# Expert stage with a fixed order on three engines, weights split five pieces ahead, halves summed and experts scattered in pairs

## The chip, the cores and the metric

The kernel runs on one core of one Trainium2 chip. The metric is the device time of one execution in microseconds; the kernel before took 2125.14 us, the median of three runs (2124.23 to 2125.2).

## The reference, cut to what matters

Two transformer blocks run one after the other on 512 tokens of width 1024. The change touches the expert layer of the first block: 16 experts, each of which takes the 64 tokens with the highest affinity to it.

```python
cap = CAPACITY_FACTOR * S // N_EXPERTS                     # 64
aff = softmax(h @ w_router)                                # per token over experts
g, idx = lax.top_k(aff.transpose(0, 2, 1), cap)
xin = h[idx]                                               # (16, 64, 1024)
a = xin @ w_gate[e];  u = xin @ w_up[e]                    # 1024 x 1024 each
y = (silu(a) * u) @ w_down[e]
y = y * g
x = x + g2 * zeros.at[idx].add(y)                          # scatter back
```

The other parts are a Fourier and windowed attention mixer before it, and behind it two further layers with other attention forms and convolutional feed-forward networks.

## The kernel before

Everything is fp32. A product that must keep fp32 accuracy on TensorE is made of fp32r matmuls on split operands: an operand is copied to `hi` (ScalarE, a cast to fp32r) and the residue `lo` is the original less `hi` (VectorE). `pieces` (L350) does this for a streamed weight: it takes a chunk of 1 MB (2048 columns on 128 partitions) that `fetch` (L337) brings from HBM on SP's queue into a raw buffer, and yields it in two pieces of 128 x 1024, each split into `whi` (L374) and `wlo` (L375). The split buffers come from the lists `parts` and by default from the pool `wp` (three); the raw buffers from the list `rings`.

The expert stage is `phase_b` (L1003). `_moe_order` gives the order of the 48 products: for each expert e a gate product (g), an up product (u) and a down product (d), as g0 u0 g1 d0 u1 g2 d1 u2 and so on, and at the end g15 u15 d14 d15. A product (`prod`, L1080) has eight pieces k of the contraction, two halves of 512 output columns in two PSUM banks, and a stationary operand of 128 columns: 64 with `hi` and 64 with `lo` of the expert's 64 rows. So the output has 128 rows, the upper half and the lower half of which are to be added. For seven of the pieces there are four matmuls (L1095: two halves, `whi` and `wlo`). Piece 5 (`WHOLE`) is not split: it is multiplied in fp32 (L1092), and its raw buffer is held until TensorE has used it.

Between the pieces of a product stand hooks, each a step of some other work: `gather` fetches the rows of the next expert by an indirect transfer, transposes them (L1072) and splits them; `activ` transposes the gate and up rows of an expert with a duplicating matmul (L1125), applies silu (L1128), multiplies (L1129, tile `sg`) and splits to `act`; `scatter` multiplies the rows `y` by the one-hot matrix `ph` (L1169) and adds the result into `x` (L1172). `first` (L1102) copies the output of a gate or up product to SBUF (L1110). `down` (L1140) scales the 128 output rows by the affinity and by g2 (`mt`, L1151), splits them to `y`, and builds `ph` (L1154), for each expert. As both halves of the 128 rows carry the same token index, the one-hot matmul adds them. The scatter goes over two experts at a time: eight steps of four matmuls and one add each.

All instructions are traced in program order, and a planner then orders those of each engine by its own estimate of when their inputs are ready. `pin` (L291) fixes an instruction behind the one traced before it on its engine; in this stage only the splits of the first three pieces are pinned. Up to the first down product there are three pairs of split buffers, then five. There are nine raw buffers (`NRAW` = 7 and two of `wp`).

Of the kernel before, what the change touches and what calls it, by code (L numbers as in the profile page):

```python
# [2 lines left out]

# [6 lines left out]
F32 = mybir.dt.float32  # L10
F32R = mybir.dt.float32r
# [4 lines left out]
OP = mybir.AluOpType  # L16
# [4 lines left out]
S = 512  # L21
D = 1024
EPS = 1e-6
NEG = -1e30
NE = 16
CAP = 64
# [1 line left out]
NF = DFF // 128  # L28
SEGS = ((0, 11), (11, 22))
CW = 2048  # L30
NPRE, NRAW, NPART = 6, 7, 2
WHOLE = (5,)
ROUTE = ((), (0,), (0, 1), (0, 1, 2, 3, 1, 2, 3, 2, 3))
SIDE = ()
NFIRST = 4
TAIL = 4
FILL = (0, 2, 2, 3, 3, 2, 2, 2, 0, 0, 0)
ODD = ("v0 v1 d0 d0 d0 d0 d0 d0 d0 d0 s0 d1 s0 d1 s0 d1 d0 d1 d1 s0 d1 s1 s0 d1 d1 s1 d1 s1 s1 s1").split()
# [221 lines left out]
    return {n: np.ascontiguousarray(v, dtype=f) for n, v in c.items()}  # L260

class Kernel:
# [737 lines left out]
    def phase_b(self, er, ep, after):  # L1003
        nc, tc, sp = self.nc, self.tc, self.sp
# [52 lines left out]
        nc.gpsimd.memset(xfull, 0.0)  # L1057
        nc.gpsimd.memset(afull, 0.0)

        def gather(e):  # L1060

# [16 lines left out]
                        nc.scalar.copy(xfull[:, e % 2, n, :CAP], t[:, k % 4])  # L1078
                yield

        def prod(name, stat, full, hooks):

            ps = [self.mm() for _ in range(2)]
            k = 0
            for j in range(4):
                for w in self.pieces(name, 1024, [i - 2 * j for i in WHOLE]):
                    for gen in hooks.get(k, ()):
                        next(gen, None)
                    for half in range(2):
                        sl = slice(half * 512, half * 512 + 512)  # L1090
                        if k in WHOLE:
                            nc.tensor.matmul(ps[half], full[:, WHOLE.index(k)], w[:, sl], start=(k == 0), stop=(k == 7))  # L1092
                            continue
                        for q in range(2):
                            nc.tensor.matmul(ps[half], stat[:, k], w[q][:, 0, sl],  # L1095
                                             start=(k + q == 0), stop=(k == 7 and q == 1))
                    k += 1
            return ps

        asb = {}  # L1100

        def first(t, e, hooks):  # L1102
            ps = prod(t, *xs[e], hooks)
            if t == "g":
                d = pw.tile([128, D], F32, name="ag", bufs=1)
            else:
                d = self.nrm.tile([128, D], F32, name="xn", tag="xn")
            asb[t, e] = d
            for half in range(2):
                nc.scalar.copy(d[:, half * 512:half * 512 + 512], ps[half])  # L1110

        act = {}

        def activ(e):
            a = [asb.pop((t, e)) for t in "gu"]
# [20 lines left out]
        ys = {}  # L1136

        def down(e, hooks):
            nonlocal pm, iota
            ps = prod("d", *act.pop(e), hooks)  # L1140
# [18 lines left out]
        def scatter(es, c):  # L1159

            for half in range(2):
                sl = slice(half * 512, half * 512 + 512)
                ps = self.av()
                n = 0
                for e in es:
                    y, ph = ys[e]
                    for q in range(2):
                        n += 1
                        nc.tensor.matmul(ps, ph[:, c * 128:(c + 1) * 128], y[:, q, sl], start=(n == 1),  # L1169
                                         stop=(n == 2 * len(es)))  # L1170
# [4 lines left out]
        def scatters(es):  # L1175
            for c in range(4):
                yield from scatter(es, c)

        gath, acts, none = gather(0), None, iter(())
        for _ in range(3):  # L1180
            next(gath)
        scat = none
# [12 lines left out]
        self.table()  # L1195
        nxt = after()
        for c in range(4):
            list(scatter([NE - 2, NE - 1], c))
            nxt(c)


# [587 lines left out]
```

## Time and profile before

| | |
|---|---|
| median of three runs | 2125.14 us (2124.23 to 2125.2) |
| the profiled execution | 2122.88 us |
| its span, first to last instruction | 2121.1 us |
| mean granted TensorE clock | 0.979 |
| TensorE matmul busy | 2006.7 us, 95% |
| VectorE busy | 1377.4 us, 65% |
| ScalarE busy | 1055.5 us, 50% |
| HBM | 169 GB/s over the span |

Busy time is the share of the span in which an engine has an instruction running; a matmul's end is modelled. In the rows, L and a number is the line of the kernel, "out<-in" are the names of tiles, x and a number counts instructions. An idle time stands before the arrow that names what ended it.

### The profile page before, as it was taken

The numbers are of one execution on the slowest core, as the hardware profiler recorded it, in microseconds if no ns is written. First come the engines' busy times: TensorE is split into PE (matmuls) and PEld (weight loads), VectorE is DVE, ScalarE is ACT, GpSimd is POOL, SyncE is SP. The second block draws the span as 40 slices with busy tenths as digits, with TensorE's granted clock in tenths as the row PEclk, the third lists the DMA queues.
The fourth block names the chain that finished last, engine by engine and source line by source line (L and its number), as shares of the span: only waits on it lengthen the run. The fifth ranks groups of instructions, "written<-read, shape, count | busy, mean of one in ns | idle before, by whom it ended". The sixth has DMA issues, their size and how long they took to land.

```text
span 2121.1 us, 24893 instructions
## 1 busy us (share of the span) xinstructions
PE 2006.7 (95%) x9331; PEld 1563.3 (74%) x9331; DVE 1377.4 (65%) x2328; ACT 1055.5 (50%) x1826; POOL 151.0 (7%) x146
## 2 busy tenths in 40 slices
PE   6889779999999999999999999999999989999998
PEld 5668657766666666787778888888887768888886
DVE  7676479888888888826856643553546776634653
ACT  3334368766777667526645433443425654423432
POOL 2003400000000010100101000001100010000001
PEclk9899989999999999999999999999999999999999
DMA  7744758999999997221123222222321023222221
GB/s 289 201 160 152 288 222 357 380 345 341 343 347 340 350 353 276 97 77 49 42 86 113 80 89 100 99 95 75 112 90 60 21 90 119 88 99 93 89 95 55
DMA packets 53932, 358.30 MB, mean 169 GB/s; under 512 B 6694, under 2 KB 7262, under 8 KB 14004
## 3 DMA queue, kind: packets, MB, share of 16 engines
q1 hardware_dynamic: 48148, 338.60, 42.7%
q0 software_dynamic: 5664, 18.12, 3.1%
q8 instruction: 73, 1.20, 0.2%
q14 instruction: 47, 0.39, 0.1%
HBM read 353.28 MB, written 4.46 MB: 169 GB/s over the span
## 4 chain that ended last, share of the span: by engine, by line
PE 82%; DVE 8%; issue 5%; ACT 3%; DMA 2%; POOL 0%; SPq 0%; DVEq 0%; POOLq 0%; ACTq 0%
PE mm L1095 15%; PE mm L384 13%; PE mm L385 13%; PE mm L386 13%; PE mm L1092 4%; PE tp L1125 2%; DVE wlo L375 2%; PE av L1169 2%; PE av L386 2%; PE av L384 2%; PE av L385 2%; PE tp L386 2%; PE tp L385 2%; PE tp L384 2%; PE mm L1220 1%
## 5 line engine op out<-in xcount | busy, mean ns | idle before, releaser
L375 DVE TENSOR_TENSOR wlo<-wraw,whi 128x1024 fp32r<-128x1024 f32 (+1 forms) x545 | 646.8, 1213 | 435.6 <-ACT whi L374 434.1
L374 ACT CAST whi<-wraw 128x1024 fp32r<-128x1024 f32 (+1 forms) x545 | 548.6, 1044 | 379.2 <-PE mm L385 148.5
L384 PE MATMUL mm<-hT_hi,whi 128*128 128x512 f32 (+1 forms) x960 | 375.9, 393 | 6.1 <-ACT whi L374 6.0
L385 PE MATMUL mm<-hT_lo,whi 128*128 128x512 f32 (+1 forms) x960 | 375.3, 392 | 0.4 <-DVE hT_lo L390 0.4
L386 PE MATMUL mm<-hT_hi,wlo 128*128 128x512 f32 (+1 forms) x960 | 374.6, 391 | 0.0
L384 PEld LDWEIGHTS mm<-hT_hi,whi 128*128 128x128 f32 x960 | 182.4, 191 | 48.8 <-ACT whi L374 6.8
L385 PEld LDWEIGHTS mm<-hT_lo,whi 128*128 128x128 f32 x960 | 182.4, 190 | 42.0 <-DVE hT_lo L390 1.6
L386 PEld LDWEIGHTS mm<-hT_hi,wlo 128*128 128x128 f32 x960 | 182.3, 190 | 40.5
L1095 PE MATMUL mm<-wlo,xs 128*128 128x512 f32 x448 | 164.6, 419 | 7.7 <-DVE wlo L375 7.7
L1095 PE MATMUL mm<-whi,xs 128*128 128x512 f32 x448 | 170.3, 429 | 0.4 <-ACT whi L374 0.4
L385 PE MATMUL mm<-wlo,hT_hi 128*128 128x512 f32 (+2 forms) x288 | 110.4, 384 | 1.1 <-DVE wlo L375 0.9
L384 PE MATMUL mm<-whi,hT_hi 128*128 128x512 f32 (+2 forms) x288 | 110.6, 386 | 0.0
L386 PE MATMUL mm<-whi,hT_lo 128*128 128x512 f32 (+2 forms) x288 | 109.4, 381 | 0.6 <-DVE hT_lo L390 0.6
L1095 PEld LDWEIGHTS mm<-wlo,xs 128*128 128x128 f32 x448 | 77.8, 190 | 42.0 <-DVE wlo L375 28.3
L1095 PEld LDWEIGHTS mm<-whi,xs 128*128 128x128 f32 x448 | 83.7, 191 | 26.8 <-issue 8.4
L1169 PE MATMUL av<-y,ph 128*128 128x512 f32 x256 | 84.6, 427 | 12.1 <-ACT y L389 11.3
L389 ACT CAST aT_hi<-cv 128x512 fp32r<-128x512 f32 x44 | 27.3, 620 | 117.0 <-DVE cv L1698 117.0
L1095 PE MATMUL mm<-wlo,act 128*128 128x512 f32 x224 | 81.1, 425 | 3.8 <-DVE wlo L375 3.6
L1095 PE MATMUL mm<-whi,act 128*128 128x512 f32 x224 | 81.8, 427 | 0.0
L1169 PEld LDWEIGHTS av<-y,ph 128*128 128x128 f32 x256 | 48.7, 192 | 38.6 <-ACT y L389 21.6
L1697 ACT ACTIVATE cv<-cv 128x512 f32<-128x512 f32 x44 | 27.8, 632 | 89.1 <-DVE cv L1694 89.1
L384 PE MATMUL av<-whi,aT_hi 128*128 128x512 f32 x176 | 69.3, 394 | 0.0
(487 smaller groups left out, 3319.4 us busy)
## 6 DMA issues: line engine op xcount, KB each, us to landing
wraw<-in_wts SPq DMA_DIRECT2D x310, 1024.0 KB, 5.6
wraw<-in_wts SPq DMA_DIRECT2D x8, 768.0 KB, 4.2
x<-in_x SPq DMA_DIRECT2D x4, 512.0 KB, 12.7
out<-x SPq DMA_DIRECT2D x4, 512.0 KB, 2.6
wraw<-in_wts SPq DMA_DIRECT2D x2, 832.0 KB, 5.4
bias<-t5scr POOLq DMA_DIRECT2D x8, 192.0 KB, 13.2
hd<-xn POOLq DMA_DIRECT2D x3, 512.0 KB, 3.2
mod<-md POOLq DMA_DIRECT2D x1, 1024.0 KB, 11.3
```

The source lines that it names most:

```text
L374: i1 = nc.scalar.copy(hi[:, :n], t[:, a:a + n])
L375: i2 = nc.vector.tensor_tensor(lo[:, :n], t[:, a:a + n], hi[:, :n].bitcast(F32), op=OP.subtract)
L384: mm(ps, a[0], b[0], start=start, stop=False)
L385: mm(ps, a[0], b[1], start=False, stop=False)
L386: mm(ps, a[1], b[0], start=False, stop=stop)
L389: self.nc.scalar.copy(hi, src)
L1092: nc.tensor.matmul(ps[half], full[:, WHOLE.index(k)], w[:, sl], start=(k == 0), stop=(k == 7))
L1095: nc.tensor.matmul(ps[half], stat[:, k], w[q][:, 0, sl], start=(k + q == 0), stop=(k == 7 and q == 1))
L1125: nc.tensor.matmul(pt[:, k * 128:(k + 1) * 128], src[:, f * 128:(f + 1) * 128], dup, start=True, stop=True)
L1169: nc.tensor.matmul(ps, ph[:, c * 128:(c + 1) * 128], y[:, q, sl], start=(n == 1), stop=(n == 2 * len(es)))
L1220: nc.tensor.matmul(ps[:, :W], lhs[:, i * 128:(i + 1) * 128], rhs[:, :W], start=True, stop=True)
L1697: nc.scalar.activation(u[0], u[0], AF.Silu)
```

## The change

The stage runs through a wrapper (`InOrder`) that pins every instruction of TensorE, VectorE and ScalarE: each of the three has the order in which the program is traced. A single stream of pieces (`feed`) now runs over all 48 products, and `piece` takes from it so that `ahead` pieces past the current one have been split: two until the first down product is done, then five, across the ends of products. The split buffers are then six pairs (three of `pm`, three of `wp`), the raw buffers seven.

A down product's two halves of 64 rows are summed: ScalarE copies the one half to the other's partitions (`ya`), VectorE adds. Two experts, an even and an odd one, stand in the upper and lower 64 rows of one tile `yt`. `pair` scales that tile (once, 1024 columns), builds one `ph` and splits one `y` for the two, in two steps that are hooks of the next up product. The scatter takes one or two pairs at a time (`GROUPS`), with two matmuls per pair and step. `activ` uses the `av` banks for its second half. The hooks move: `activ` to pieces 2 and 3 of the gate product, the scatter to 5 and 7, in the up product to 3 and 7 where no pair is being finished.

```diff
-NPRE, NRAW, NPART = 6, 7, 2
+NPRE, NRAW, NPART = 6, 5, 3
+AHEAD = 5
+GROUPS = {1: (0, 1), 3: (2, 3), 5: (4, 5), 6: (6,), 7: (7,)}
...
+        idxp, gp = (sp.tile([128, NE // 2], F32, name=n, bufs=1) for n in ("idxp", "gp"))
+        for i in range(2):
+            h = slice(i * CAP, i * CAP + CAP)
+            nc.vector.tensor_copy(idxp[h], idxT[h, i::2])
+            nc.vector.tensor_copy(gp[h], gT[h, i::2])
...
-        self.late = 3
...
+        self.nc = nc = InOrder(nc, self.pin)
+        order = _moe_order()
+        feed = (w for t, _ in order for j in range(4) for w in self.pieces(t, 1024, [i - 2 * j for i in WHOLE]))
+        queue = []
+        ahead = 2
+
+        def piece():
+            queue.extend(itertools.islice(feed, ahead + 1 - len(queue)))
+            return queue.pop(0)
...
-            k = 0
-            for j in range(4):
-                for w in self.pieces(name, 1024, [i - 2 * j for i in WHOLE]):
-                    for gen in hooks.get(k, ()):
-                        next(gen, None)
+            for k in range(8):
+                w = piece()
+                for gen in hooks.get(k, ()):
+                    next(gen, None)
...
-                pg, pu = self.tp(), self.tp()
+                pg, pu = (self.av(), self.av()) if g else (self.tp(), self.tp())
...
-                self.parts = ([(self.wp, 3)] * 3 + [(pm, NPART)] * NPART) * 8 * NE
-                del self.parts[(3 * NE - 4) * (8 - len(WHOLE)):]
+                self.parts = ([(pm, NPART)] * NPART + [(self.wp, 3)] * 3) * 8 * NE
+                ahead = AHEAD
                 iota = self.const_load(pm, "iota")
-            y = pm.tile([128, 2, D], F32R, name="y", bufs=2)
+            own, other = (slice(i * CAP, i * CAP + CAP) for i in (e % 2, 1 - e % 2))
+            if e % 2 == 0:
+                rows[e // 2] = pm.tile([128, D], F32, name="yt", bufs=1)
+            t = rows[e // 2]
             for half in range(2):
                 sl = slice(half * 512, half * 512 + 512)
-                t = pm.tile([128, 512], F32, name="mt", bufs=2)
-                nc.vector.scalar_tensor_tensor(t, ps[half], gT[:, e:e + 1], self.g2[:, sl], op0=OP.mult, op1=OP.mult)
-                self.split(y[:, 0, sl], y[:, 1, sl], t)
-            ph = pm.tile([128, S], F32R, name="ph", bufs=2)
-            nc.vector.tensor_scalar(ph, iota, idxT[:, e:e + 1], None, op0=OP.is_equal)
-            ys[e] = (y, ph)
+                a = pm.tile([128, 512], F32, name="ya", bufs=2)
+                nc.scalar.copy(a[own], ps[half][other])
+                nc.vector.tensor_tensor(t[own, sl], ps[half][own], a[own], op=OP.add)
...
+        def pair(p, n):
+            t = rows.pop(p)
+            y = pm.tile([128, 2, D], F32R, name="y", bufs=3)
+            ph = pm.tile([128, S], F32R, name="ph", bufs=3)
+            ys[p] = y, ph
+            for i in range(n):
+                sl = slice(i * D // n, (i + 1) * D // n)
+                nc.vector.scalar_tensor_tensor(t[:, sl], t[:, sl], gp[:, p:p + 1], self.g2[:, sl], op0=OP.mult, op1=OP.mult)
+                if i == 0:
+                    nc.vector.tensor_scalar(ph, iota, idxp[:, p:p + 1], None, op0=OP.is_equal)
+                    yield
+                self.split(y[:, 0, sl], y[:, 1, sl], t[:, sl])
+            yield
...
-        for t, e in _moe_order():
+        for t, e in order:
             if t == "g":
                 gath = gather(e + 1) if e + 1 < NE else none
-                first(t, e, {0: [gath], 1: [acts or none], 3: [acts or none], 4: [scat], 5: [scat], 6: [scat], 7: [scat]})
+                first(t, e, {0: [gath], 2: [acts], 3: [acts], 5: [scat], 7: [scat]})
             elif t == "u":
-                first(t, e, {1: [scat], 2: [gath], 3: [scat], 4: [gath], 5: [scat], 7: [scat]})
+                fresh = fin is not none
+                first(t, e, {1: [fin], 2: [gath], 3: [none if fresh else scat], 4: [gath], 5: [fin],
+                             7: [none if fresh else scat]})
+                fin = none
                 acts = activ(e)
             else:
-                down(e, {1: [acts], 3: [acts]} if e + 2 == NE else {})
-                list(scat)
-                scat = scatters([e - 1, e]) if e % 2 and e + 1 < NE else none
+                down(e, {2: [acts], 3: [acts], 4: [scat], 5: [scat], 6: [scat], 7: [scat]} if e + 2 == NE else {})
+                if e % 2:
+                    p = e // 2
+                    fin = pair(p, 2 if e + 1 == NE else 1)
+                    if p in GROUPS:
+                        list(scat)
+                        scat = scatters(GROUPS[p]) if e + 1 < NE else none
+        list(fin)
```

`InOrder` hands every call of `nc.scalar`, `nc.vector` and `nc.tensor` through and pins the instruction that comes back.

## Rows read from the trace of the kernel before

**Rows 1.** windows: busy us of PE, PEld, DVE, ACT, POOL; clock; DMA; GB/s
```profile
279.40:320.80 41.40, 41.34 (x167) 29.37 (x168) 36.16 (x36) 35.56 (x47) 2.74 (x3) 0.93 0.65 251
...
458.40:533.00 74.60, 71.03 (x306) 48.79 (x304) 63.63 (x72) 51.37 (x72) 2.36 (x2) 1.00 0.93 344
...
320.80:855.10 534.30, 512.67 (x2223) 359.38 (x2221) 465.02 (x527) 375.46 (x512) 22.72 (x14) 1.00 0.90 340
325.00:425.00 100.00, 98.22 (x445) 72.61 (x444) 93.27 (x107) 76.66 (x108) 3.48 (x3) 1.00 0.96 381
```

**Rows 2.** chain of waits over two experts: start us, us, engine, line, count
```profile
552.90 0.64 PE tp L1072 x8
...
569.52 0.73 DVE mt L1151
...
573.77 1.20 PE mm L1095 x4
...
577.84 0.93 PE av L1169 x4
...
579.24 1.72 PE mm L1092 x4
580.95 2.32 PE mm L1095 x10
...
587.47 1.34 PE tp L1125 x12
```

**Rows 3.** VectorE's timeline: start us, us, instructions, idle time before
```profile
559.95 6.99 DVE L375 TENSOR_TENSOR wlo<-wraw,whi 128x1024 fp32r<-128x1024 f32 x6 [1.51 <-ACT whi L374]
...
585.13 0.42 DVE L1129 TENSOR_TENSOR sg<-sg,tp 128x256 f32<-128x256 f32 x1 [1.07 <-PE tp L1125]
585.47 1.22 DVE L375 TENSOR_TENSOR wlo<-wraw,whi 128x1024 fp32r<-128x1024 f32 x1
586.60 0.42 DVE L390 TENSOR_TENSOR act<-sg,act 128x256 fp32r<-128x256 f32 x1
```

**Rows 4.** groups of instructions from 320.8 to 855.1: busy us, mean ns, idle us
```profile
L375 DVE TENSOR_TENSOR wlo<-wraw,whi 128x1024 fp32r<-128x1024 f32 x308 | 363.4, 1220 | 18.2 <-ACT whi L374 17.5
L374 ACT CAST whi<-wraw 128x1024 fp32r<-128x1024 f32 x309 | 306.5, 1051 | 22.0 <-PE mm L1095 21.3 <-DVE wlo L375 0.6
...
L1172 DVE TENSOR_TENSOR x<-x,av 128x512 f32<-128x512 f32 x56 | 38.3, 685 | 7.7 <-PE av L1169 7.6
...
L1151 DVE SCALAR_TENSOR_TENSOR mt<-mm,gT,row_g 128x512 f32<-128x512 f32 x30 | 21.1, 747 | 15.1 <-PE mm L1095 15.1
...
L389 ACT CAST y<-mt 128x512 fp32r<-128x512 f32 x30 | 18.1, 618 | 16.4 <-DVE mt L1151 16.1
...
L389 ACT CAST act<-sg 128x256 fp32r<-128x256 f32 x30 | 12.2, 406 | 17.0 <-DVE sg L1129 16.9
...
L1154 DVE TENSOR_SCALAR ph<-c_iota,idxT 128x512 fp32r<-128x512 f32 x16 | 7.2, 482 | 0.0
```

**Rows 5.** waits of SP's transfer queue from 320.8 to 855.1: total, times, longest
```profile
SPq L345 <- DVE wlo L375: 295.5, 125, 8.9
SPq L345 <- PE mm L1092: 119.9, 43, 5.4
```

**Rows 6.** groups of instructions, whole span, of the shapes nearest to the new ones
```profile
L457 DVE SCALAR_TENSOR_TENSOR x<-osb,rs_y,x 128x1024 f32<-128x1024 f32 x16 | 21.3, 1331 | 0.8
...
L1365 DVE TENSOR_TENSOR qT<-mm,c_ropeq 64x512 f32<-64x512 f32 x8 | 5.6, 694 | 1.0 <-ACT qT L1364 0.8
...
L1364 ACT COPY qT<-mm 64x512 f32<-64x512 f32 x8 | 4.6, 576 | 2.6 <-PE mm L386 2.5
```

**Rows 7.** timeline at the stage's end, VectorE and TensorE
```profile
855.12 1.41 DVE L1151 SCALAR_TENSOR_TENSOR mt<-mm,gT,row_g 128x512 f32<-128x512 f32 x2 [0.97 <-PE mm L1095]
...
856.57 0.49 PE L1169 MATMUL av<-y,ph 128*128 128x512 f32 x1 [1.26 <-ACT y L389]
```

**Rows 8.** transfers issued from 320.8 to 855.1, KB each, median us to landing
```profile
wraw<-in_wts SPq DMA_DIRECT2D x167, 1024.0 KB, 7.0
```

More of the change, by code (lines that the diff above doesn't have):

```diff
@@ L1 @@
+import itertools
 import math
@@ L260, in constants, with __init__, __getattr__, pinned @@
     return {n: np.ascontiguousarray(v, dtype=f) for n, v in c.items()}
+class InOrder:
+    class Engine:
+        def __init__(self, engine, pin):
+            self.engine, self.pin = engine, pin
+        def __getattr__(self, name):
+            op = getattr(self.engine, name)
+            def pinned(*a, **k):
+                ins = op(*a, **k)
+                self.pin(ins)
+                return ins
+            return pinned
+    def __init__(self, nc, pin):
+        self.nc = nc
+        self.scalar, self.vector, self.tensor = (self.Engine(e, pin) for e in (nc.scalar, nc.vector, nc.tensor))
+    def __getattr__(self, name):
+        return getattr(self.nc, name)
 class Kernel:
@@ L1058, in phase_b @@
         nc.gpsimd.memset(afull, 0.0)
+        plain = nc
+        self.nc = nc = InOrder(nc, self.pin)
[6 more added lines that the diff above has]
+            return queue.pop(0)
         def gather(e):
@@ L1079, in gather, with prod @@
                 yield
-        def prod(name, stat, full, hooks):
+        def prod(stat, full, hooks):
             ps = [self.mm() for _ in range(2)]
-            k = 0
-            for j in range(4):
-                for w in self.pieces(name, 1024, [i - 2 * j for i in WHOLE]):
-                    for gen in hooks.get(k, ()):
-                        next(gen, None)
[L1089 to L1097, printed above, removed]
+            for k in range(8):
+                w = piece()
+                for gen in hooks.get(k, ()):
+                    next(gen, None)
+                for half in range(2):
+                    sl = slice(half * 512, half * 512 + 512)
+                    if k in WHOLE:
+                        nc.tensor.matmul(ps[half], full[:, WHOLE.index(k)], w[:, sl], start=(k == 0), stop=(k == 7))
+                        continue
+                    for q in range(2):
+                        nc.tensor.matmul(ps[half], stat[:, k], w[q][:, 0, sl],
+                                         start=(k + q == 0), stop=(k == 7 and q == 1))
             return ps
@@ L1102, in first @@
         def first(t, e, hooks):
-            ps = prod(t, *xs[e], hooks)
+            ps = prod(*xs[e], hooks)
             if t == "g":
@@ L1136, in phase_b @@
         ys = {}
+        rows = {}
         def down(e, hooks):
-            nonlocal pm, iota
-            ps = prod("d", *act.pop(e), hooks)
+            nonlocal pm, iota, ahead
+            ps = prod(*act.pop(e), hooks)
             if pm is None:
@@ L1143, in down, with scatter @@
                 pm = self.pool(er, "b_m", side="right")
-                self.parts = ([(self.wp, 3)] * 3 + [(pm, NPART)] * NPART) * 8 * NE
-                del self.parts[(3 * NE - 4) * (8 - len(WHOLE)):]
+                self.parts = ([(pm, NPART)] * NPART + [(self.wp, 3)] * 3) * 8 * NE
+                ahead = AHEAD
                 iota = self.const_load(pm, "iota")
-            y = pm.tile([128, 2, D], F32R, name="y", bufs=2)
+            own, other = (slice(i * CAP, i * CAP + CAP) for i in (e % 2, 1 - e % 2))
+            if e % 2 == 0:
+                rows[e // 2] = pm.tile([128, D], F32, name="yt", bufs=1)
+            t = rows[e // 2]
             for half in range(2):
                 sl = slice(half * 512, half * 512 + 512)
-                t = pm.tile([128, 512], F32, name="mt", bufs=2)
-                nc.vector.scalar_tensor_tensor(t, ps[half], gT[:, e:e + 1], self.g2[:, sl], op0=OP.mult, op1=OP.mult)
-                self.split(y[:, 0, sl], y[:, 1, sl], t)
-            ph = pm.tile([128, S], F32R, name="ph", bufs=2)
-            nc.vector.tensor_scalar(ph, iota, idxT[:, e:e + 1], None, op0=OP.is_equal)
-            ys[e] = (y, ph)
-        iota = None
-        def scatter(es, c):
+                a = pm.tile([128, 512], F32, name="ya", bufs=2)
+                nc.scalar.copy(a[own], ps[half][other])
+                nc.vector.tensor_tensor(t[own, sl], ps[half][own], a[own], op=OP.add)
+        iota = None
+        def pair(p, n):
[11 more added lines that the diff above has]
+            yield
+        def scatter(ps_, c):
             for half in range(2):
@@ L1164, in scatter @@
                 n = 0
-                for e in es:
-                    y, ph = ys[e]
+                for p in ps_:
+                    y, ph = ys[p]
                     for q in range(2):
@@ L1169, in scatter @@
                         nc.tensor.matmul(ps, ph[:, c * 128:(c + 1) * 128], y[:, q, sl], start=(n == 1),
-                                         stop=(n == 2 * len(es)))
+                                         stop=(n == 2 * len(ps_)))
                 xc = self.x[:, c, sl]
@@ L1173, in scatter, with scatters @@
                 yield
-        def scatters(es):
+        def scatters(ps_):
             for c in range(4):
-                yield from scatter(es, c)
-        gath, acts, none = gather(0), None, iter(())
+                yield from scatter(ps_, c)
+        none = iter(())
+        gath, acts = gather(0), none
         for _ in range(3):
             next(gath)
-        scat = none
-        for t, e in _moe_order():
+        scat = fin = none
+        for t, e in order:
             if t == "g":
                 gath = gather(e + 1) if e + 1 < NE else none
-                first(t, e, {0: [gath], 1: [acts or none], 3: [acts or none], 4: [scat], 5: [scat], 6: [scat], 7: [scat]})
+                first(t, e, {0: [gath], 2: [acts], 3: [acts], 5: [scat], 7: [scat]})
             elif t == "u":
-                first(t, e, {1: [scat], 2: [gath], 3: [scat], 4: [gath], 5: [scat], 7: [scat]})
+                fresh = fin is not none
+                first(t, e, {1: [fin], 2: [gath], 3: [none if fresh else scat], 4: [gath], 5: [fin],
+                             7: [none if fresh else scat]})
+                fin = none
                 acts = activ(e)
             else:
-                down(e, {1: [acts], 3: [acts]} if e + 2 == NE else {})
-                list(scat)
-                scat = scatters([e - 1, e]) if e % 2 and e + 1 < NE else none
+                down(e, {2: [acts], 3: [acts], 4: [scat], 5: [scat], 6: [scat], 7: [scat]} if e + 2 == NE else {})
[6 more added lines that the diff above has]
+        list(fin)
+        self.nc = nc = plain
+        self.parts = []
         el.close()
@@ L1197, in phase_b @@
         for c in range(4):
-            list(scatter([NE - 2, NE - 1], c))
+            list(scatter(GROUPS[NE // 2 - 1], c))
             nxt(c)
```

## The prediction

> **What bounds the kernel now.** I read the page's engine shares first, then the windows, the chain of waits over two experts, VectorE's timeline and the groups of instructions, and last the waits of SP's transfer queue. By the table of the profile TensorE is busy for 95% of the span, but a matmul's end is modelled, so this says little; the expert stage has to be taken apart. It runs from 279.4 to 855.1 us; 41.4 us go to the first four products, and 534.3 us to the other 45, that is 35.6 us per expert (three products), with a steady 74.6 us for two experts [rows 1]. The granted clock is 1.00 (the 2.4 GHz level) from 320.8 us on and 0.93 on average before; nothing in the change bears on it.
>
> TensorE needs less than that. From the chain [rows 2]: ten matmuls of a product take 2.32 us, so 0.232 each; the four of an unsplit piece 1.72; four scatter matmuls 0.93; twelve duplicating matmuls 1.34; eight gather transposes 0.64. Per expert: 84 x 0.232 = 19.5, 3 x 1.72 = 5.2, 32 x 0.112 = 3.6, 0.6, and 16 scatter matmuls x 0.2325 = 3.7 (3.5 in this window, as the last pair comes later): 32.4 us. So 3.2 us per expert are waits. Where they lie, the chain shows: a product ends at 569.5, and the path runs over VectorE (the scaled rows mt, a weight residue, y, again a residue) to 573.8, where the next product goes on [rows 2].
>
> VectorE is next. Six residues in a row take 6.99 us, so one is 1.15 us when one follows another, although its own time is 1.22 [rows 3, 4]. The last overlaps its successor by some 0.07 to 0.1 us, so I take 0.60 for an add of 0.685 into x and 0.34 for a 256-column operation of 0.42 [rows 3, 4]. Per expert: 21 x 1.15 = 24.2; adds into x 56/15 x 0.60 = 2.2; mt 2 x 0.70, y's residue 2 x 0.65 (its form is that of the add) and ph 0.44 (0.48 less the overlap) = 3.1 [rows 4]; six 256-column operations 2.0: 31.5 us. The windows say 465.0 / 15 = 31.0 [rows 1]. Both engines lie within a tenth of 35.6, and since the lead of the split is short they lose time to each other in turn: VectorE stands idle when a product's end is awaited, and TensorE while VectorE catches up.
>
> The transfers are third: 340 GB/s over the window, 344 in steady state at 0.93 of the transfer engines' time, 381 at 0.96 in the best 100 us [rows 1]. SP stood 295.5 us waiting for a residue to free a buffer and 119.9 us for an unsplit piece's matmul [rows 5], so they are paced by buffers now, though not far from their own limit.
>
> **Scatter by fours, two experts in one set of rows.** In this window 7 pairs x 16 instead of 14 x 16 scatter matmuls: 112 x 0.2325 = 26 us off TensorE, 1.7 per expert, leaving 30.6. Adds into x fall from 56 to 32 in the window: 24 x 0.60 = 14 us off VectorE.
>
> **Summing the halves.** Per expert two ScalarE copies of 64x512 and two VectorE adds of 64x512 come in. The nearest rows are a 64x512 copy from PSUM at 0.576 and a 64x512 two-input operation from PSUM at 0.694 [rows 6]; fewer partitions do not make them shorter, so I take 0.60 in a row for the add. Bounds: 0.35 (what a 256-column one takes in a row) to 0.75 (mt). Per pair there remain one 128x1024 scaling, one ph, one residue: 1.33 as in the nearest row [rows 6], 0.44, 1.15 = 2.9, or 1.5 per expert. VectorE pays 1.2 + 1.5 = 2.7 instead of 3.1. With the adds into x (32/15 x 0.60 = 1.3): 24.2 + 1.3 + 2.7 + 2.0 = 30.2 us per expert. ScalarE goes up by 2 x 0.5 + 0.5 - 2 x 0.6 = 0.3 on 375.5 / 15 = 25.0 [rows 1]: no bound.
>
> **The lead.** With six split buffers, ScalarE can begin piece k+5 when TensorE is done with k-1, and it is ready 1.05 + 1.22 = 2.3 us later [rows 4]; TensorE gets there after 5 x 0.93 = 4.65 us. That leaves 2.4 us and more. At a product's end ScalarE's copies wait for TensorE as before, but five pieces are ready by then. This hides the 4.3 us hole of [rows 2]; most of the 3.2 us per expert can go.
>
> **The fixed order.** It has a price where VectorE and ScalarE hand one tile to and fro. Now a residue stands between the gated product and its low part: sg at 585.13, a residue at 585.47, act at 586.60 [rows 3]. After the change these two are neighbours: the ScalarE cast between (0.41 [rows 4]) is awaited, and the next piece's cast stands behind it on ScalarE (1.05), of which act covers 0.42. Twice per expert: 0.45 + 0.6 and, with a further small copy, 0.45 + 0.85: 2.4 us. What is queued behind on VectorE are the residues that TensorE will need five pieces on. So VectorE goes from 30.2 to 32.6 us per expert when it is the late one, and nothing when it is ahead. A second price: the scatter bank taken at step 5 of a gate product is one that the gated products used at step 3. If VectorE is late there (after an up product in which a finished pair costs it 2.9 us extra), TensorE waits for it; I put that at 3 us in two of four experts, bounds 0 and 4, and 30.6 + 1.5 = 32.1 is still below VectorE's 32.6.
>
> The rule that speaks against this is in the Trainium skill, TensorE: Matmul & The Clock Gate, section on the array's architectural detail: VectorE and ScalarE take their queue strictly in order. The trace agrees as far as it goes: the idle time before sg stands in one piece, with the residue that could have filled it behind it [rows 3]. By that rule alone each such wait is paid in full, which is the 32.6 above; without it the sum would be 30.6.
>
> **Transfers and buffers.** Raw buffers fall from 9 to 7, while the split empties them five pieces earlier; only the chunk with the unsplit piece is held until TensorE uses it. 340 GB/s x 534.3 us is 181.7 MB, 12.1 MB per expert. At 381 GB/s [rows 1] that is 31.8 us, at 381 / 0.96 = 397 it is 30.5, at 344 / 0.93 = 370 it is 32.7. A transfer lands 7.0 us after its issue [rows 8], with a new one every 3 us (169 in 534.3), so two or three of the seven buffers are under way: no stall of its own, but no room either.
>
> **The sum.** VectorE 32.6, transfers 30.5 to 32.7, TensorE 30.6 to 32.1 per expert, all within a few per cent. Before, 32.4 and 31.5 made 35.6. I take 33.2: 0.6 on the largest, a fifth of the 3.2 that was lost before. Gain (35.6 - 33.2) x 15 = 36 us. Against it: the first four products keep three split buffers and a lead of two, now with the act price: +2 (0 to 5). At the end the last pair passes ScalarE copy, add, add, scaling and cast (0.58 + 0.69 + 0.69 + 0.75 + 0.62 = 3.3 us [rows 4, 6]) before its first scatter matmul, where now it takes 1.45 (855.12 to 856.57 [rows 7]); 16 matmuls fewer give part back: +1.5 (0 to 3). The four small index copies lie in VectorE's wait for the first gather. Outside the stage nothing changes. Net -32.5 us. The profiled execution took 2122.9 us (span 2121.1 and 1.8 around it), so it would be 2090.4; the median of the runs lies 2.2 above it: 2093 us. A stage at 32.4 to 34.4 per expert gives 2080 to 2111.
>
> **Rivals.**
> TensorE alone bounds. If the lead absorbs every wait, an expert costs 31.2: 15 x 4.4 = 66, net -63, 2062 us. For it: 2.4 us of slack per piece. Against it: VectorE's 30.2 leaves 1.0 us for waits of which I count 2.4.
>
> Transfers bound. With seven buffers and bursts of three behind the held chunk they may not exceed 350 GB/s: 12.1 / 0.350 = 34.6, net -11, 2114 us; it decides once VectorE and TensorE fall below 34.6. For it: the share of 0.93 at only 344 GB/s. Against it: 381 over 100 us, and SP's waits for buffers. The Trainium skill, DMA: Bandwidth & Descriptors, Specifications, gives some 358 GB/s as the HBM limit of a core; by that it would be 33.8 us and 2102. The trace does not agree that this is a ceiling: 381 over 100 us.
>
> Slower: the fixed order makes TensorE wait in every gate product. If VectorE is more than two pieces late at step 5, TensorE stands for 4 us in each, loses the lead, and the act price is paid again by TensorE at the next up and down products (1.5 each): 30.6 + 7 = 37.6, +30 and +3.5, 2159 us. It decides from 35.6 - 30.6 = 5.0 us of waits per expert on. Against it: the up product that precedes a gate has only two of four pairs' finishing work.
>
> **Chances.** Forecast 0.59, TensorE alone 0.15, transfers 0.15, slower 0.11. About 0.2% (4 us) is what a measurement tells from none. The forecast's cases and TensorE's are all faster; a fifth of the transfers' case and some of the forecast's upper end come near none. Faster 0.84, same 0.05, slower 0.11. The range for eight in ten reaches from TensorE's case, 2060, to the poorer half of the transfers' one, 2121.
>
> **What would show it.** After the stage's start, L1095 no longer waits 3 to 4 us at a product's end; the period of two experts falls from 74.6 to about 66 us; VectorE's adds of halves are near 0.69 each; the transfers rise to some 370 to 385 GB/s; the idle time before VectorE's act and the residue after it grows. Wrong if VectorE has over 5 us of idle time per expert, if the residues wait for transfers, or if the stretch from the first down product's end to the last is above 525 us.

## The result, and the profile after

The changed kernel takes 2097.49 us (median of 4 runs, 2095.03 to 2099.54) against 2124.68 (4 runs, 2122.32 to 2125.2): ratio 0.9872, 95% interval [0.9857, 0.9888], so 27 us faster; 2093 was forecast, in a range of 2060 to 2121. The profiled execution took 2099.54 us with a span of 2097.8, 23.3 less than before. Cut at the same events as [rows 1], the span of after minus that of before is: up to the first matmul of the stage +1.5 (280.9 against 279.4; over the profiled executions of all the kernels here, this start lay between 276.4 and 285.2, so it says nothing of the change), first four products +3.0, the other 45 products -34.6, everything behind the last product +6.8.

In the rows PE is TensorE, PEld its weight loads, DVE VectorE, ACT ScalarE, POOL GpSimd and SPq the queue of transfers. The windows of after that answer to [rows 1]: start to end, then span of the window and busy us of TensorE, its weight loads, VectorE, ScalarE, GpSimd; granted clock, DMA share, GB/s. The first is the first four products, the second the other 45, the third four experts.
```profile
280.90:325.30 44.40, 43.12 (x168) 29.04 (x169) 36.18 (x35) 35.24 (x45) 2.30 (x2) 0.93 0.56 205
325.30:825.00 499.70, 474.51 (x2114) 353.51 (x2112) 445.34 (x479) 380.50 (x521) 28.69 (x20) 0.98 0.94 371
461.30:596.70 135.40, 129.28 (x577) 97.12 (x576) 121.09 (x131) 104.04 (x143) 6.79 (x4) 0.97 0.95 377
```
An expert takes 499.7 / 15 = 33.3 us; two take 67.7, not 74.6. VectorE works 445.3 / 15 = 29.7 of the 33.3, so it is idle for 3.6.

The groups of instructions of the same 499.7 us (count, busy us, mean ns, idle time before and what ended it) answer to [rows 4, 6]. L279 is the line of the wrapper that pins every call of the stage, so groups go by tiles.
```profile
L279 DVE TENSOR_TENSOR wlo<-wraw,whi 128x1024 fp32r<-128x1024 f32 x307 | 360.0, 1219 | 39.1 <-ACT whi L279 37.4
...
L279 DVE TENSOR_TENSOR x<-x,av 128x512 f32<-128x512 f32 x32 | 21.7, 680 | 0.0
...
L279 DVE TENSOR_TENSOR yt<-mm,ya 64x512 f32<-64x512 f32 x30 | 19.3, 682 | 0.2
...
L279 ACT COPY ya<-mm 64x512 f32<-64x512 f32 x30 | 16.0, 581 | 0.8 <-PE mm L279 0.4
...
L279 DVE TENSOR_TENSOR act<-sg,act 128x256 fp32r<-128x256 f32 x30 | 12.8, 425 | 14.1 <-ACT act L279 14.1
...
L279 DVE SCALAR_TENSOR_TENSOR yt<-yt,gp,row_g 128x1024 f32<-128x1024 f32 x7 | 8.9, 1276 | 0.0
```
The adds into x are 32 instead of 56, the copies and adds of halves cost 0.58 and 0.68 us, the scaling of a pair 1.28. Of VectorE's 54.4 us of idle time, 51.5 end with a cast of ScalarE (37.4 + 14.1): they hand tiles to each other, and one stands.

The waits of after in the same window (total, times, longest), for [rows 5] and against what was forecast of the scatter bank:
```profile
ACT xfull L279 <- DVE xs L279: 54.6, 14, 5.3
ACT act L279 <- DVE sg L279: 44.2, 30, 2.1
DVE wlo L279 <- ACT whi L279: 37.4, 49, 1.2
...
PE tp L279 <- ACT xn L279: 21.0, 9, 3.0
...
PEld av L279 <- ACT sg L279: 0.8, 2, 0.5
...
SPq L372 <- DVE wlo L279: 186.4, 99, 12.0
SPq L372 <- PE mm L279: 184.0, 42, 8.9
```
The first row was not foreseen; before the change the same wait, from 320.8 to 855.1, was
```profile
ACT xfull L1078 <- DVE xs L390: 8.1, 5, 1.6
```
`gather` splits the transposed rows (`xs`: a cast on ScalarE, a residue on VectorE) and then lets ScalarE copy one column group of the same PSUM tile to `xfull`. In the program that copy waits for the residue. In the fixed order the residue stands in VectorE's queue behind work that is late, and behind the copy in ScalarE's queue stand `y`, the next casts, and the copy of the up product's rows, `xn`. The chain of waits of after (start us, us, what) shows one passage; it is what has come in the place of [rows 2]'s hole at 569.5.
```profile
565.56 1.11 DVE yt L279
...
568.40 0.42 DVE xs L279
568.82 2.27 DVE wlo L279 x2
571.09 0.34 DVE xs L279
...
571.46 0.02 ACT xfull L279
...
572.52 0.76 ACT y L279
...
573.46 1.99 ACT whi L279 x2
575.45 0.49 ACT xn L279
...
575.99 1.16 PE tp L279 x8
```
TensorE lives on its five split pieces in the meantime, and then stands at the duplicating matmuls that read `xn`: 21.0 us in 9 places. The same passage two experts on, in the timeline (the idle time before in brackets) and in windows of 2 us:
```profile
644.59 1.31 PE L279 MATMUL tp<-c_dup,xn 128*128 128x128 f32 x8 [2.46 <-ACT xn L279]
...
642.00:644.00 2.00, 0.14 (x2) 0.00 (x0) 2.00 (x3) 2.00 (x4) 0.00 (x0) 1.00 1.00 377
644.00:646.00 2.00, 1.41 (x9) 1.41 (x10) 1.88 (x2) 2.00 (x5) 0.00 (x0) 0.87 1.00 414
646.00:648.00 2.00, 2.00 (x7) 1.61 (x7) 2.00 (x2) 1.20 (x2) 0.00 (x0) 0.50 1.04 434
648.00:650.00 2.00, 2.00 (x16) 2.00 (x15) 1.12 (x3) 1.27 (x3) 0.00 (x0) 0.78 0.99 410
```
After 2.46 us of standing the granted clock falls from 1.00 to 0.50 (1.2 GHz), and TensorE gets 7 matmuls done in those 2 us; the next 2 us, at 0.78, hold 16. This happens six times in the stage, and nowhere in the stage before the change.

The end of the stage, [rows 7], in the timeline of after (start us, us, instruction, idle time before):
```profile
826.47 1.30 DVE L279 TENSOR_TENSOR yt<-mm,ya 64x512 f32<-64x512 f32 x2
827.81 0.75 DVE L279 SCALAR_TENSOR_TENSOR yt<-yt,gp,row_g 128x512 f32<-128x512 f32 x1
828.14 1.80 POOL L1358 MEMSET qz<- 64x2048 f32 x1
828.48 1.74 DVE L279 TENSOR_SCALAR ph<-c_iota,idxp 128x512 fp32r<-128x512 f32 x1
...
830.37 0.76 PE L1227 MATMUL av<-y,ph 128*128 128x512 f32 x1 [5.04 <-DVE ph L279]
...
841.98 1.32 PE L462 MATMUL tp<-ident,xn 128*128 128x128 f32 x8 [1.49 <-DVE xn L476]
```
From the last product to the first scatter matmul 5.4 us pass (1.5 before), and to the first transposes of the next part 17.0, where before these are 10.2 us behind 855.1:
```profile
865.30 0.60 PE L435 MATMUL tp<-ident,xn 128*128 128x128 f32 x4
```
So all of the +6.8 arises here. For [rows 8]: 169 transfers of 1 MB (167 before), now with a median of 9.4 us to landing instead of 7.0. The transfer queue still stands for buffers, 186.4 us for residues and 184.0 for matmuls of a product.

### The profile page after: what moved, and what is told of

It reads as the page before. It is cut to its first block, busy times and chain, and to the rows that moved or that the text cites. A ratio compares the mean times of both kernels' runs of the same rounds, so it can differ in the third digit from the quotient of the medians.

```text
span 2097.8 us, 24799 instructions
## 1 busy us (share of the span) xinstructions
PE 1966.8 (94%) x9203; PEld 1554.2 (74%) x9203; DVE 1362.1 (65%) x2286; ACT 1060.8 (51%) x1835; POOL 153.3 (7%) x146
## 4 chain that ended last, share of the span: by engine, by line
PE 76%; DVE 10%; issue 6%; ACT 5%; DMA 3%; POOL 0%; SPq 0%; ACTq 0%; DVEq 0%; POOLq 0%
PE mm L279 13%; PE mm L411 13%; PE mm L412 13%; PE mm L413 13%; DVE wlo L279 3%; PE av L279 2%; PE av L413 2%; PE av L412 2%; PE av L411 2%; PE tp L411 2%; PE tp L413 2%; ACT whi L279 2%; PE tp L412 2%; DMA wraw<-in_wts 2%; PE mm L1289 1%
## 5 line engine op out<-in xcount | busy, mean ns | idle before, releaser
L402 DVE TENSOR_TENSOR wlo<-wraw,whi 128x1024 fp32r<-128x1024 f32 (+2 forms) x209 | 250.6, 1201 | 412.2 <-ACT whi L401 412.1
L279 DVE TENSOR_TENSOR wlo<-wraw,whi 128x1024 fp32r<-128x1024 f32 x336 | 393.9, 1219 | 46.1 <-ACT whi L279 44.3
L401 ACT CAST whi<-wraw 128x1024 fp32r<-128x1024 f32 (+2 forms) x209 | 214.8, 1030 | 356.5 <-PE mm L412 145.3
L279 ACT CAST whi<-wraw 128x1024 fp32r<-128x1024 f32 x336 | 333.1, 1050 | 15.8 <-PE mm L279 14.8
L412 PEld LDWEIGHTS mm<-hT_lo,whi 128*128 128x128 f32 x960 | 182.3, 190 | 41.2 <-DVE hT_lo L417 1.6
L279 PE MATMUL mm<-whi,xs 128*128 128x512 f32 x448 | 199.7, 446 | 2.3 <-ACT whi L279 2.3
L279 PE MATMUL mm<-wlo,xs 128*128 128x512 f32 x448 | 183.1, 409 | 4.0 <-DVE wlo L279 3.7
L279 PEld LDWEIGHTS mm<-wlo,xs 128*128 128x128 f32 x448 | 86.6, 193 | 36.5 <-DVE wlo L279 14.5
L279 PEld LDWEIGHTS mm<-whi,xs 128*128 128x128 f32 x448 | 86.8, 194 | 27.3 <-issue 6.2
L279 PE MATMUL mm<-whi,act 128*128 128x512 f32 x224 | 94.4, 422 | 0.0
L279 PE MATMUL mm<-wlo,act 128*128 128x512 f32 x224 | 89.3, 399 | 0.5 <-DVE wlo L279 0.5
L411 PE MATMUL tp<-whi,aT_hi 128*128 128x512 f32 x176 | 69.4, 395 | 0.0
```

The lines of the kernel that those rows point to most:

```text
L279: ins = op(*a, **k)
L401: i1 = nc.scalar.copy(hi[:, :n], t[:, a:a + n])
L402: i2 = nc.vector.tensor_tensor(lo[:, :n], t[:, a:a + n], hi[:, :n].bitcast(F32), op=OP.subtract)
L411: mm(ps, a[0], b[0], start=start, stop=False)
L412: mm(ps, a[0], b[1], start=False, stop=False)
```

## Experiments

Ratios are to the kernel before, with their 95% intervals; the medians of before beside them lay between 2122.27 and 2124.93. "Stage" is the stretch of the 45 products, cut as above. "Theory" and "rival" are the two outcomes set out before each run.

**1. The xfull copy first.** In `gather`:
```
             t = pt[:, :4 * CAP].rearrange("p (k c) -> p k c", k=4)
-            self.split(st[...], t)
             for n, k in enumerate(WHOLE):
                 ... nc.scalar.copy(xfull[...], t[:, k % 4])
+            self.split(st[...], t)
```


> The changed kernel with one edit: ScalarE's small copy of the unsplit piece's rows (xfull) is traced ahead of the split of the same PSUM tile, not behind it. Theory (what is still lost in the stage is ScalarE standing behind VectorE's xs residue in its fixed order, and TensorE then standing for the up product's copy): ScalarE's 54.6 us of waits before xfull go, TensorE's 22 us before the duplicating matmuls on xn fall under 4, the granted clock no longer drops to 0.50 inside the stage, and the time falls by 20 to 32 us, to about 2070. Rival 1 (VectorE's own work sets the pace): the waits move, the time stays within 8 us of 2097. Rival 2 (transfers set the pace at 381 GB/s): the same, with waits for wraw in their place.

2075.43 us (2071.93 to 2079.42), 0.979 [0.9774, 0.9806]; stage 479.5, 32.0 per expert, one fall of the clock in it.
```profile
320.50:800.00 479.50, 466.15 (x2113) 344.73 (x2111) 443.14 (x479) 381.01 (x521) 30.03 (x20) 1.00 0.98 387
```
Its waits that are of interest:
```profile
ACT act L279 <- DVE sg L279: 65.5, 30, 5.2
...
PEld av L279 <- ACT sg L279: 12.0, 7, 2.2
```
The theory held but for one fall of the clock that stayed: two lines of program order were worth 20 us of the stage. About 8 of them are matmuls that run faster (TensorE's busy time is 466.2 us instead of 474.5, for the same work and with one fall of the clock instead of six); about 12 are time in which it stood. What is left is the act hand-over, and now the scatter-bank wait of the prediction appears, 12.0 us on the weight loads in 7 places and 8.9 on the matmuls behind them.

**2. The fixed order with a lead of two.** `-AHEAD = 5`, `+AHEAD = 2`.

> The changed kernel with a lead of two pieces (AHEAD = 2) to the end, everything else as changed. Theory (the lead of five fills the product ends): each product end waits again for a cast and a residue, 1 to 2 us over 45 products; 2097 + 45 to 90 = 2140 to 2190, slower than the kernel before. Rival (less scatter and add work made the gain, the lead nothing): 2097 to 2105.

2120.59 us (10 runs, 2115.0 to 2125.86), 0.9987 [0.9973, 1.0001]; stage 521.6. Of the theory only the direction held: in this order the lead is worth 23 us, half of the least that the theory said and three times the most that the rival said.

**3. The planner's order instead of the fixed one.**
```
-        self.nc = nc = InOrder(nc, self.pin)
+        self.late = 3
+        self.nc = nc = InOrder(nc, lambda ins: None)
```


> The changed kernel without the pins: the same instructions, but the planner orders TensorE, VectorE and ScalarE (only the first three splits pinned, as before). Theory (the fixed order carries the lead, and costs some waits): the planner puts evacuations ahead of splits again, product ends wait, 2105 to 2125. Rival (the fixed order only costs; the smaller work made the gain): 2070 to 2092.

2086.51 us (2085.59 to 2092.54), 0.9834 [0.9818, 0.9851]; stage 496.2, no fall of the clock in it.
```profile
326.40:822.60 496.20, 476.51 (x2098) 337.60 (x2096) 443.44 (x480) 377.69 (x519) 17.80 (x19) 1.00 0.96 373
```
The theory was wrong: as the change stands, the fixed order costs 11 us against the planner's by the medians (8 by the ratios): 3.5 in the stage, 3 in the first products (41.2 to 41.3 us in every run of the planner's order, 43.3 to 45.1 in every fixed one), 4.6 behind the last product.

**4. Single experts in the fixed order.** The old `down` and the old scatters, pairs and halves undone:
```
-                nc.scalar.copy(a[own], ps[half][other])
-                nc.vector.tensor_tensor(t[own, sl], ps[half][own], a[own], op=OP.add)
...
+                nc.vector.scalar_tensor_tensor(t, ps[half], gT[:, e:e + 1], self.g2[:, sl], op0=OP.mult, op1=OP.mult)
+                self.split(y[:, 0, sl], y[:, 1, sl], t)
+            nc.vector.tensor_scalar(ph, iota, idxT[:, e:e + 1], None, op0=OP.is_equal)
```


> The changed kernel with the old end of a down product: each expert's 128 rows scaled, split and scattered by themselves (two experts per group, eight steps of four matmuls and one add), in the fixed order and with the lead of five. Theory (VectorE and TensorE share the limit, 32.6 and 32.1 per expert): TensorE gets 26 us more, VectorE about 1.3 us per expert: 2115 to 2123. Rival (the lead alone made the gain, TensorE and VectorE have room): 2097 to 2104.

2148.72 us (2145.11 to 2152.66), 1.0123 [1.0107, 1.014]; stage 553.6. I had hung the first scatter step at piece 3 of the up product, too early: TensorE waited there for `ph` itself.
```profile
PEld av L279 <- ACT whi L279: 32.9, 7, 4.8
PE av L279 <- DVE ph L279: 30.0, 7, 4.4
```
So it does not measure the pairs; run 9 does.

**5. Runs 1 and 3 together** (the copy first, planner's order).

> Planner's order (no pins) with the xfull copy traced first. Theory (the wait for xfull is a fault of the fixed order alone; the planner put the copy elsewhere): no gain over the planner's order without it, 2083 to 2092, some 10 us slower than the fixed order with xfull first (2075). Rival (the planner's order is better in itself by some 11 us, as it was without the edit): 2062 to 2070.

2085.25 us (2081.92 to 2088.71), 0.9825 [0.9806, 0.9844]; stage 496.7. No gain over run 3, as the theory said: the xfull wait is a price of the fixed order alone. In run 3's stage ScalarE has no wait for `xs` before `xfull` at all.

**6. Runs 2 and 3 together** (lead of two, planner's order): of the change remain pairs, halves, hooks and the buffers' split.

> Planner's order (no pins), lead of two pieces in the traced order, summed halves and pairs as changed. It shows what the pairs bring without fixed order and lead. Theory (the lead is worth some 23 us in either order): 2105 to 2115. Rival (the planner looks ahead by itself, the traced lead means nothing to it): 2083 to 2092.

2088.16 us (2087.36 to 2089.18), 0.9835 [0.9818, 0.9852]; stage 496.8. TensorE's wait for a weight residue in the stage, before the change, after it and in this run:
```profile
PE mm L1095 <- DVE wlo L375: 11.3, 19, 0.6
...
PE mm L279 <- DVE wlo L279: 3.2, 9, 0.5
...
PE mm L279 <- DVE wlo L279: 18.8, 27, 1.7
```
The rival held. Pairs and halves with their hooks and buffers make 35 us without lead or fixed order; the program-order lead is nothing where the planner orders ScalarE and VectorE (run 3, with a lead of five in the program, has 18.3 us of this wait in 28 places). What the single stream of pieces, the buffers' split and the moved hooks are worth apart from the pairs was not tried.

**7. The last pair half by half** (with run 1): in `down` of the last expert, `ph` ahead of the product and for each half
```
+                if last:
+                    nc.vector.scalar_tensor_tensor(t[:, sl], t[:, sl], gp[...], self.g2[:, sl], ...)
+                    self.split(y[:, 0, sl], y[:, 1, sl], t[:, sl])
```


> The kernel with xfull first, and the last pair's end rearranged: its one-hot matrix ph is built before the last down product, and each half of 512 columns is scaled and split as soon as it is summed. Theory (TensorE's 5.0 us wait at the stage's end, with ph at 1.74 us in its path, and the low clock that follows it are the 6.7 us lost behind the last product): 2075 less 3 to 7, 2068 to 2072. Rival (the end is bound by the norm's chain behind it): 2074 to 2076.

2078.01 us (2072.25 to 2081.8), 0.9777 [0.9754, 0.9799]; nothing gained where the theory had 3 to 7 us, and the first transposes of the next part still come 17.0 us behind the last product. ScalarE's timeline shows a reason: the copy of the second half stands behind the first half's cast, which waits for VectorE. Run 11 takes it up.
```profile
806.30 0.58 ACT L279 COPY ya<-mm 64x512 f32<-64x512 f32 x1
...
809.82 0.62 ACT L279 CAST y<-yt 128x512 fp32r<-128x512 f32 x1 [2.02 <-DVE yt L279]
810.46 0.58 ACT L279 COPY ya<-mm 64x512 f32<-64x512 f32 x1
```
**8. Half of the transfers** (with run 1): of each chunk of the stage's weights half the columns are loaded, and both pieces use them; the kernel leaves the other half out.
```
+        n = w // 2 if self.chunks[pos][0] == "B" else w
-        ins = self.nc.sync.dma_start(t[:, :w], ...)
+        ins = self.nc.sync.dma_start(t[:, :n], ...)
```


> The kernel with xfull first, in which the expert stage loads only half of every weight chunk and uses that half for both pieces: half the transfers of the stage, all else the same (the output is not the reference's). Theory (VectorE and TensorE set the pace, transfers are hidden up to some 395 GB/s): 2070 to 2076, ScalarE's 6.4 us of waits for wraw gone. Rival (transfers set the pace by now): 2050 or less.

2075.33 us (2074.16 to 2076.8), 0.9771 [0.9754, 0.9788]; stage 479.5 at 200 GB/s, as long as run 1's at 387. The theory held: transfers do not bound run 1, and so not the change at 371.

**9. Single experts with a late scatter and the copy first.** Run 4 with run 1's edit; scatter steps only from the last piece of the up product on.

> The kernel with xfull first, with the old end of a down product (each expert scaled, split and scattered by itself, groups of two experts), in the fixed order with the lead of five; the scatter starts only at the last piece of the up product behind the pair, so that no matmul waits for a one-hot matrix just begun. Theory (summed halves and pairs are the main source of the gain; the planner's order with them and a lead of two gained 35): 2075 + 26 to 40 = 2101 to 2115. Rival (the 51 us of the first such run were mostly its own early scatter): 2080 to 2095.

2120.49 us (9 runs, 2118.51 to 2123.25), 0.9977 [0.9966, 0.9987]; stage 527.3, 35.2 per expert. Against run 1 the pairs and halves are worth 45 us by the medians (40 by the ratios, 48 in the stage), at or above the upper end of the theory's 26 to 40. ScalarE stands for VectorE's scaled rows after every down product:
```profile
ACT y L279 <- DVE mt L279: 61.6, 30, 3.1
```
**10. The act hand-over spread over two hooks** (with run 1): between the gated product and its split now lies one piece.
```
                 nc.vector.tensor_tensor(sg, sg, pu..., op=OP.mult)
+                yield
                 self.split(st[...], st[...], sg)
-                first(t, e, {0: [gath], 2: [acts], 3: [acts], ...
+                first(t, e, {0: [gath], 2: [acts], 3: [acts, acts], 4: [acts], ...
```
and `sg` gets two buffers; the hooks of the down product d14 move alike.

> The kernel with xfull first, with a step more between the gated product and its split, so that the next piece's cast and residue stand between them in the fixed order (sg has two buffers). Theory (ScalarE's 65.5 us of waits for sg and VectorE's 2.4 us per expert behind them hold the stage above TensorE's 30.6 per expert): 2075 less 5 to 15, 2060 to 2070. Rival (32.0 per expert is set by TensorE and the scatter's banks; the waits are idle time that costs nothing): 2073 to 2078.

2069.37 us (2065.91 to 2070.22), 0.973 [0.9709, 0.9752]; stage 468.1, 31.2 per expert. The theory held: 11.4 us of the stage, 6 of the medians (in its profiled execution the stage's start, which varies, lies 8.2 us later than in run 1's). ScalarE's wait for `sg` goes from 65.5 us to 14.5, and a new row comes up:
```profile
ACT whi L279 <- DMA wraw<-in_wts: 28.9, 46, 2.2
...
ACT act L279 <- DVE sg L279: 14.5, 24, 3.0
```
**11. Run 10 with a new end.** `ph` ahead of the last product, then both copies (these ahead of the sums in every down product), then sum, scaling and cast half by half, the residues last:
```
+            for sl, a, b in hs:
+                nc.vector.tensor_tensor(t[own, sl], b[own], a[own], op=OP.add)
+                if last:
+                    nc.vector.scalar_tensor_tensor(t[:, sl], t[:, sl], gp[...], self.g2[:, sl], ...)
+                    nc.scalar.copy(y[:, 0, sl], t[:, sl])
```


> As the run before it, and the last pair's end rearranged once more: the one-hot matrix before the last product, both copies of halves first, then sum, scaling and cast half by half. Theory (at the stage's end ScalarE's second copy stood behind the first half's cast): 2 to 5 us below the run before it. Rival (the end is bound by what the next stage's queue holds): within 2 us of it.

2060.53 us (2059.09 to 2064.57), 0.9698 [0.9677, 0.9719]: the fastest kernel here, 64 us below before.
```profile
323.50:790.40 466.90, 461.42 (x2113) 345.23 (x2111) 443.27 (x480) 386.56 (x521) 38.53 (x20) 1.00 1.00 397
```
The first transposes of the next part come 13.2 us behind the last product (790.4), 3.4 us earlier than in run 10 (16.6). The medians lie 8.8 us apart, more than the 2 to 5 of the theory. The spans of the two profiled executions lie 9.5 apart, and of these 3.4 are this end, 1.2 the stage, 0.5 the first four products and 4.4 the stage's start (280.2 against 284.5), which lies ahead of the edit: so about half of the difference is shown to be the edit's.

**12. Half of the transfers in run 11**, as in run 8.

> The run with spaced steps and the end rearranged, again with only half of every weight chunk of the stage loaded and used twice (the output is not the reference's). In that run ScalarE waited 28.9 us for wraw in 46 pieces. Theory (TensorE's 30.6 us per expert is the floor, 31.1 is reached, and the lead of five hides those waits): 2057 to 2063. Rival (transfers begin to bind at 31 us per expert, some 400 GB/s): 2045 to 2054.

2053.08 us (2051.04 to 2056.22), 0.9674 [0.9655, 0.9692]; stage 461.5 instead of 466.9. The theory missed and the rival held: at 397 GB/s and a DMA share of 1.00 the transfers have begun to bind, though only by 5 (stage) to 7 us (medians).

## Why the prediction was right in size and wrong in parts

**The terms of VectorE.** The work was forecast as 30.2 us per expert and is 29.7; the adds came at 0.68 us, the scaling at 1.28. The act price was put at 2.4 us per expert on VectorE. In run 1, where the xfull wait is gone, VectorE is busy for 443.1 of 479.5 us, so it stands for 36.4 / 15 = 2.4 us; 14.1 of the 36.4 are before `act` in 30 places, 20.3 before residues that wait for a cast, in 34. Spreading the hand-over (run 10) takes the wait before `act` away and leaves (468.1 - 443.0) / 15 = 1.7. In one place of the profile after, the parts of the forecast, 0.45 and 0.6 to 0.85, are 0.47 and 0.52:
```profile
612.91 0.42 DVE L279 TENSOR_TENSOR sg<-sg,tp 128x256 f32<-128x256 f32 x1
613.80 0.42 DVE L279 TENSOR_TENSOR act<-sg,act 128x256 fp32r<-128x256 f32 x1 [0.47 <-ACT act L279]
614.75 1.23 DVE L279 TENSOR_TENSOR wlo<-wraw,whi 128x1024 fp32r<-128x1024 f32 x1 [0.52 <-ACT whi L279]
```
So the step that counted a hand-over in the fixed order was sound, and by run 10 the wait is in the path, not only idle time. These waits agree with the rule of the Trainium skill that VectorE and ScalarE take their queues strictly in order (TensorE: Matmul & The Clock Gate, the section on the array's architectural detail).

**The stage's sum of 33.2 met 33.3 partly by luck.** The 0.6 "on the largest" stood for waits in general. In the trace the largest wait is another hand-over of the same kind, that of `xfull`, which I did not look for: the prediction followed VectorE's queue and never listed what stands behind a waiting copy on ScalarE. Run 1 prices it at 20 us of the stage, 1.3 per expert; without it the stage would have come out at 32.0, below the forecast. The prediction also held the clock to be out of it ("nothing in the change bears on it"): it fell six times in the stage, each time after TensorE stood, and about 8 of those 20 us are matmuls at the lower clock. Two readings were off without weight in the sum: VectorE's 31.0 us lay an eighth below 35.6, not within a tenth, and the transfers in the window were 167, not 169.

**Why the gain is there.** The forecast put it on two things, less work by pairs and a lead that hides the product-end hole; "most of the 3.2 us per expert can go" was said of the lead. That step failed as a cause. Run 6, with neither lead nor fixed order, has a stage of 496.8 and gains 35 us; in the fixed order the pairs are worth 40 to 45 (run 9 against run 1) and the lead 23 (run 2), but order and lead together, as the change has them, cost 9 (run 6), the order alone 11 (run 3). The fixed order pays once the copy stands first: run 1 is 10 us below run 5, which has the same edit in the planner's order. Run 11 is 25 below run 5, but its further edits were not tried in the planner's order. Why fewer scatter steps take waits away beyond their own work (about 26 us of TensorE in the forecast) has a candidate only in the fixed order, the wait in the row of run 9, which no run takes away by itself; in the planner's order it is left open.

**The scatter bank.** TensorE was to wait 3 us in two of four experts, 22 us in the stage. It waits 21.0 us in 9 places, but for `xn`, in the duplicating matmuls that come ahead of the scatter; the bank wait proper is 0.8 us on the weight loads. The size is a coincidence: with the `xn` wait gone (run 1) the bank wait is 12.0 there and 8.9 on the matmuls.

**Transfers.** Forecast 370 to 385 GB/s, measured 371 and 377. That they would bind at 350 or less is refuted by run 8 (no time gained by halving them at 387) and placed by run 12, at 397. The 358 GB/s that the Trainium skill gives for a core (DMA: Bandwidth & Descriptors, Specifications) is not a ceiling in these traces: 397 over 467 us.

**The first four products** cost +3.0 (forecast +2, 0 to 5).

**The stage's end is the mis-sized term**: +1.5 (0 to 3) was forecast, +6.8 measured, though with 16 matmuls fewer, as forecast. The chain of copy, adds, scaling and cast was right; what was left out is that `ph` stands behind the scaling in the fixed order and takes 1.74 us there, that weight residues of the next part stand between, and that TensorE, after 5.04 us of standing, does the scatter at a granted clock of 0.50 to 0.62 (before, the scatter had 0.61 from 859.1 to 863.1 and 1.00 from there on):
```profile
829.00:833.00 4.00, 1.55 (x2) 0.57 (x2) 3.78 (x5) 0.76 (x2) 1.68 (x2) 0.60 0.41 174
833.00:837.00 4.00, 3.53 (x8) 2.36 (x8) 2.41 (x5) 2.23 (x3) 0.00 (x0) 0.50 0.00 0
837.00:841.00 4.00, 3.49 (x8) 1.50 (x6) 3.33 (x9) 3.44 (x11) 0.21 (x1) 0.62 0.00 0
```
To the next part's first transposes run 10 takes 16.6 us, run 3 in the planner's order 12.9, run 11 13.2. How the rest splits between `ph`, the residues and the clock was not tried. The net was forecast as -32.5 in the spans and came out at -23.3: 5.3 of the difference of 9.2 lie here, 1.5 in the start, 1.0 in the first four products, 1.4 in the stage.

**The rivals.** TensorE alone (31.2 per expert, 2062) is what run 11 reaches (31.1 and 2060.53) and the change does not; run 12, at 461.5 / 15 = 30.8, comes to within 0.2 of the 30.6 that the forecast counted for TensorE. The slower case stands at waits above 5.0 us per expert; the change has 33.3 - 30.6 = 2.7 on TensorE by the forecast's count, and run 4, with 553.6 / 15 = 36.9, shows that a scatter step hung too early makes the fixed order slower than before, though with single experts, whose matmuls take 32.4 by the same count.

## To carry to other kernels

Before an order is fixed, list for each pair of engines every tile that goes to and fro, and what stands behind each waiting instruction on both queues, the small copies too; a 0.21 us copy behind another engine's residue cost 20 us here. Compare with the same work in the planner's order before crediting the fixed order with the gain. At the end of a stage, order the queue so that what the next engine needs comes first, and look at the clock that it will then have.

## What was not expected of the hardware

- Standing for 2.5 us in a stage in which TensorE is busy for 95% was followed by a granted clock of 0.50; the 5.04 us at the end by 0.50 to 0.62 for 12 us. In run 1, which stands less, the clock fell once in the stage.
- `ph` (128x512, from SBUF) took 1.74 us where GpSimd's memsets of 64x2048 (1.80 each) ran beside it, and 0.48 in [rows 4]. That the memsets are the cause was not tried.
- Loads of 1 MB ran at 397 GB/s over 467 us (run 11), above the 381 of the best 100 us before.
